# Passages between the parts of a decoder layer in a written order, with the output projection run one token tile after the other

## The chip, the cores and the metric

The kernel runs on one core of a Trainium2 chip. The metric is the device time of one execution in microseconds (us); for the kernel before there are three timed runs and one profiled execution. The engines are named as in the profile: PE (TensorE, matrix products and transposes), DVE (VectorE), ACT (ScalarE), POOL (GpSimd) and SP (SyncE, which issues the loads).

## The reference, cut to what matters

A trunk of two decoder layers on 256 tokens with model width 1024 in float32.

```python
def hybrid_layer(x, ...):
    h = rms_norm(x, attn_pre_gain)
    u = h @ w_in                                  # 1024 -> 4120 columns
    o_a = swa_sink_attention(qa, ka, va, sinks)   # from the columns of u
    o_b = nsa_attention(...)                      # compressed, selected, window
    mixed = sigmoid(g_a) * (o_a @ w_branch_a) + sigmoid(g_b) * (o_b @ w_branch_b)
    x = x + rms_norm(mixed @ w_out, attn_post_gain)
    h = rms_norm(x, ffn_pre_gain)
    x = x + rms_norm(conv_ffn(h, ffn_w_up, conv_w, conv_b, ffn_w_down), ffn_post_gain)
    return x

def conv_ffn(h, w_up, conv_w, conv_b, w_down):    # d_ff = 2816
    u = h @ w_up                                  # 1024 -> 2 * 2816
    c = conv_b + sum(conv_w[k] * (u shifted by 2 - k tokens) for k in range(3))
    a, val = split(c, 2)
    return (gelu(a) * val) @ w_down
```

rms_norm(x, g) is x * rsqrt(mean(x * x) + eps) * g. The change concerns three places: from `mixed @ w_out` to the FFN's up-projection, the last columns of the FFN, and from the FFN's end to the next layer's `h @ w_in`.

## The kernel before, in words

The 256 tokens are two tiles t of 128, which lie on the partitions. The residual stream X stays on chip. Every float32 factor is split into a hi part (rounded to the matmul's format, a copy on ACT, L114) and a lo part (the rest, a subtraction on DVE, L117), and each product is three matmuls that add up in one PSUM bank: hi x hi, hi x lo and lo x hi (`mm3`, L376 to L378). A normalised activation is transposed by PE in groups of four 128x128 blocks (`t4`, L383), and the transposed tile is split in the same way.

All weights pass once through a stream `W`. A chunk is 512 KB: SP loads it into one of four slots "st", ACT makes hi, DVE makes lo. hi and lo go into the rings "wh" and "wl" of four slots each, or into other homes that happen to be free: "kB" (one), "sg" (two), "q8" (three). `W.next` hands out the next chunk and makes chunks ahead of use by the number `ahead` of each; `W.make(i)` makes a certain one early, and `W.high(i)` makes the hi part and returns the function for the lo part.

PSUM has eight banks under four names, two each: "mm", "S", "O", "T". In tiles of the profile's rows the name stands without its number.

The program is written part by part (`part`), and `later(n, fn)` puts work n parts later. Within it a scheduler sets each engine's order, except in blocks under `tc.manual_schedule`, where the engines keep the written order. What matters here, layer by layer:

- `out_layer`, the output projection: 8 chunks k of w_out, 128 rows by 1024 columns; for each chunk and tile six matmuls into two banks (`res[0]` is O, `res[1]` is S). `post_norm` and `after` make the mean square on ACT (L372), the gain on DVE (L401), rstd on POOL (L364, L365), X on DVE (L407), the mean square of X, X times the next gain (L974), rstd again, and the scaled rows xg (L981). `t8` transposes xg into the pair `hp` of "q8" homes.
- `ffn_layer`: the first two column pairs are computed with tokens on the partitions (`up_first`, four chunks into a bank "mm" for each tile) and transposed. The other pairs j = 2 to 21 have the columns on the partitions (`up`, L1022 to L1024, 24 matmuls of 256 columns for each of two halves), then the convolution (L1007 to L1009), gelu (L1031), the product (L1035), its split, and `down` with LAG pairs' delay: six matmuls for each tile into S (t = 0) and O (t = 1).
- At the end of the FFN the products of pairs 18 to 21 remain for both tiles. w_down chunks 20 and 21 lie in "kB" and "sg", 18 and 19 in the ring. Then `post_norm`, `gained` (L415) and the transposes to the next layer's `xp`, and `in_tile(0)` with its four chunks of w_in.

The order of the output projection's products before (t, k), with tile 0's last two between tile 1's first ones:

```python
order = [(0, k) for k in range(6)] + [(1, 0), (1, 1), (0, 6), (1, 2), (0, 7), (1, 3), (1, 4), (1, 5), (1, 6), (1, 7)]
```

Of the kernel before, what the change touches and what calls it, by code (L numbers as in the profile page):

```python
# [65 lines left out]
def tile_hybrid_trunk(  # L66
# [49 lines left out]
    def sub(dst, a, b):  # L116
        dve.tensor_tensor(dst, a, b, ALU.subtract)  # L117
# [270 lines left out]
    def t8(src, pair, t):  # L388
        tk = slice(t * P, (t + 1) * P)
        for h in range(2):  # L390
            t4(src[:, h * 512:(h + 1) * 512], pair[0][:, h * 4:h * 4 + 4, tk], pair[1][:, h * 4:h * 4 + 4, tk])

    def behind(ins):
        return nullcontext() if ins is None else tc.issue_after(ins.ins)

    def post_norm(t, banks, gain, follow=None, after=None):
        s2 = mean_sq(banks)
# [1 line left out]
        with behind(after):
            for n in range(2):  # L400
                dve.tensor_tensor(g[n], banks[n], gain[:, n * 512:(n + 1) * 512], ALU.mult)  # L401
        r = rstd_of(s2)
        last = None
        for n in range(2):
            xs = X[:, t, n * 512:(n + 1) * 512]
            with behind(last):
                dve.scalar_tensor_tensor(xs, g[n], r, xs, ALU.mult, ALU.add)  # L407
            if follow:
                last = follow(n)
        return last  # L410
# [858 lines left out]
```

## Time and profile before

| | us |
|---|---|
| timed runs | 784.13, 784.28, 782.39; median 784.13 |
| profiled execution, device time | 782.81 |
| its span in the trace | 781.0 |
| busy: PE, DVE, ACT, POOL | 759.2, 613.1, 495.4, 34.0 |
| weights and inputs read | 129.37 MB, 167 GB/s over the span |

The span runs from the first to the last instruction of the profiled execution; the device time has 1.8 us around it. A row of the timeline reads: start, duration, engine, line, operation, out<-in, shape, count, and in brackets the idle time before it with what ended it. In a list of waits a row names who waited for whom, the total, the times and the longest. Matmuls overlap in the pipeline, so their spacing from start to start is their price, not the duration in the row. The granted clock of PE was 0.998.

### The profile page before, as it was taken

The page shows a single profiled execution, that of the slowest core. Times are in us where ns is not written, and L with a number is a line of the kernel's source. Part 1 is how long each engine was busy: PE and PEld are TensorE (multiplying, and loading weights), DVE is VectorE, ACT ScalarE, POOL GpSimd, SP SyncE. Part 2 cuts the span into 40 slices and gives each one's busy share as a digit, 9 for nine tenths or more (in the row PEclk, how much of TensorE's full clock was granted, in tenths as well). Part 3 has the DMA queues.
Part 4 walks back from the last instruction along what each step waited for, and adds up shares of the span by engine and source line. Part 5 has one row for each costly group of instructions (what it writes and reads, how often), then busy time and mean ns, then how long its engine had stood idle before and what let it go on. Part 6 is the DMA issues. An engine that isn't in the chain of part 4 may idle for free.

```text
span 781.0 us, 12886 instructions
## 1 busy us (share of the span) xinstructions
PE 759.2 (97%) x4742; PEld 676.8 (87%) x4742; DVE 613.1 (79%) x1188; ACT 495.4 (63%) x950; POOL 34.0 (4%) x60
## 2 busy tenths in 40 slices
PE   8999999999899999999989999999999999999996
PEld 6788898887799999999868889988878999999995
DVE  6899898686787777777787989985876877677775
ACT  6596986754665555565556969866465655566552
POOL 4300001000100000000010000010010000000000
PEclk9999999999999999999999999999999999999999
DMA  8624264465566565665545323644645556656731
GB/s 337 196 86 133 64 219 170 136 188 162 173 205 189 188 187 184 209 210 188 164 134 163 95 82 121 200 153 162 200 144 172 188 187 189 188 182 201 217 104 54
DMA packets 42346, 131.26 MB, mean 168 GB/s; under 512 B 5375, under 2 KB 5931, under 8 KB 42283
## 3 DMA queue, kind: packets, MB, share of 16 engines
q1 hardware_dynamic: 41707, 129.39, 52.0%
q10 hardware_dynamic: 576, 1.05, 0.4%
q8 instruction: 37, 0.61, 0.3%
q14 instruction: 26, 0.21, 0.1%
HBM read 129.37 MB, written 1.05 MB: 167 GB/s over the span
## 4 chain that ended last, share of the span: by engine, by line
PE 83%; ACT 8%; DVE 4%; POOL 2%; issue 1%; DMA 1%; SPq 0%; DVEq 0%; POOLq 0%; ACTq 0%
PE mm L376 6%; PE mm L378 6%; PE mm L377 6%; PE T L1024 5%; PE mm L1023 5%; PE T L1023 5%; PE mm L1024 5%; PE T L1022 5%; PE mm L1022 5%; PE S L377 5%; PE S L376 5%; PE S L378 5%; PE O L376 3%; PE O L377 3%; PE O L378 3%; ACT k L635 2%
## 5 line engine op out<-in xcount | busy, mean ns | idle before, releaser
L117 DVE TENSOR_TENSOR wl<-st,wh 128x1024 fp32r<-128x1024 f32 (+2 forms) x220 | 260.4, 1186 | 101.5 <-ACT wh L114 100.3
L114 ACT ACTIVATE wh<-st 128x1024 fp32r<-128x1024 f32 (+2 forms) x220 | 225.5, 1028 | 178.1 <-PE O L378 40.5
L376 PE MATMUL mm<-wh,x 128*128 128x512 f32 (+2 forms) x248 | 92.9, 375 | 0.7 <-DVE VT L546 0.6
L377 PE MATMUL mm<-wl,x 128*128 128x512 f32 (+2 forms) x248 | 91.6, 370 | 0.0
L378 PE MATMUL mm<-wh,x 128*128 128x512 f32 (+2 forms) x248 | 91.3, 368 | 0.1
L1023 PE MATMUL mm<-q,wh 128*128 128x256 f32 x320 | 90.7, 284 | 0.0
L1024 PE MATMUL T<-q,wl 128*128 128x256 f32 x320 | 90.6, 283 | 0.0
L1023 PE MATMUL T<-q,wh 128*128 128x256 f32 x320 | 90.6, 283 | 0.0
L1024 PE MATMUL mm<-q,wl 128*128 128x256 f32 x320 | 90.6, 283 | 0.0
L1022 PE MATMUL T<-q,wh 128*128 128x256 f32 x320 | 90.5, 283 | 0.0
L1022 PE MATMUL mm<-q,wh 128*128 128x256 f32 x320 | 90.5, 283 | 0.0
L1022 PEld LDWEIGHTS mm<-q,wh 128*128 128x128 f32 x320 | 61.4, 192 | 0.9
L1022 PEld LDWEIGHTS T<-q,wh 128*128 128x128 f32 x320 | 61.4, 192 | 0.8
L1023 PEld LDWEIGHTS mm<-q,wh 128*128 128x128 f32 x320 | 61.4, 192 | 0.8
L1023 PEld LDWEIGHTS T<-q,wh 128*128 128x128 f32 x320 | 61.4, 192 | 0.7
L1024 PEld LDWEIGHTS mm<-q,wl 128*128 128x128 f32 x320 | 61.4, 192 | 0.1
L1024 PEld LDWEIGHTS T<-q,wl 128*128 128x128 f32 x320 | 61.4, 192 | 0.0
L378 PEld LDWEIGHTS mm<-wh,x 128*128 128x128 f32 x248 | 46.7, 188 | 6.1 <-DVE x L117 0.5
L376 PEld LDWEIGHTS mm<-wh,x 128*128 128x128 f32 x248 | 46.7, 188 | 6.0 <-issue 0.8
L377 PEld LDWEIGHTS mm<-wl,x 128*128 128x128 f32 x248 | 46.7, 188 | 4.8
L635 ACT ACTIVATE k<-k,mn 128x128 f32<-128x128 f32 (+1 forms) x96 | 42.4, 445 | 7.1 <-DVE mn L632 7.0
L114 ACT ACTIVATE k<-k 128x256 fp32r<-128x256 f32 x72 | 29.1, 413 | 9.1 <-DVE k L1035 5.6
(294 smaller groups left out, 1657.0 us busy)
## 6 DMA issues: line engine op xcount, KB each, us to landing
st<-in_ffn_w_up_dram SPq DMA_DIRECT2D x88, 512.0 KB, 4.2
st<-in_ffn_w_down_dram SPq DMA_DIRECT2D x44, 512.0 KB, 3.9
st<-in_w_in_dram SPq DMA_DIRECT2D x42, 512.0 KB, 3.6
st<-in_w_out_dram SPq DMA_DIRECT2D x16, 512.0 KB, 3.8
st<-in_w_in_dram SPq DMA_DIRECT2D x16, 384.0 KB, 3.1
st<-in_cmp_w_dram SPq DMA_DIRECT2D x16, 256.0 KB, 2.6
st<-in_w_branch_a_dram SPq DMA_DIRECT2D x8, 512.0 KB, 3.6
st<-in_w_branch_b_dram SPq DMA_DIRECT2D x8, 512.0 KB, 3.5
```

The costliest lines, as they stand in the source:

```text
L114: return act.activation(dst, src, AF.Copy, scale=scale)
L117: dve.tensor_tensor(dst, a, b, ALU.subtract)
L376: pe.matmul(o, xh, wh, start=first, stop=False, skip_group_check=True)
L377: pe.matmul(o, xh, wl, start=False, stop=False, skip_group_check=True)
L378: pe.matmul(o, xl, wh, start=False, stop=last, skip_group_check=True)
L635: last_exp[0] = act.activation(self.pt[:, hh, s, :], sm[:, :nk], AF.Exp, bias=self.mn[:, i:i + 1], scale=-1.0, accum_out=self.dn[:, i:i + 1])
L1022: pe.matmul(o, wh[:, k, :], hh[:, k, c0:c1], start=(k == 0), stop=False, skip_group_check=True)
L1023: pe.matmul(o, wh[:, k, :], hl[:, k, c0:c1], start=False, stop=False, skip_group_check=True)
L1024: pe.matmul(o, wl[:, k, :], hh[:, k, c0:c1], start=False, stop=(k == 7), skip_group_check=True)
```

## The change

- The output projection runs tile 0 through all eight chunks (banks O), then tile 1 in the order 2, 0, 1, 3, 4, 5, 6, 7 (banks S). All eight chunks are kept: 5 in a new pair of homes "split" (the tiles "kA" and "vbd"), 6 in "sg", 7 in "q8". The first up-projection chunk goes into "kB" instead of "q8".
- From the second product on, PE, DVE and ACT follow the written order until the first product of tile 1 of `up_first`. The norm is written out as `norm_a`, `norm_b` and `scaled`; `scaled` does gain and rstd in one instruction. Tile 0's transposes stand behind the fifth and the sixth chunk of tile 1, tile 1's transposes behind tile 0 of `up_first` (`last_T`).
- `up_first` does hi x hi for both k of a chunk, then hi x lo, then lo x hi.
- The last pair j = 21 is taken out of the loop: its first half has the bank "T", its second a bank "mm" of its own, in written order, and so is the rest of the passage to the next layer: all products of tile 0, then tile 1's, with tile 0's transposes ahead of and behind the last chunk, and tile 1's transposes inside `in_tile(0)` of the next layer. In the last layer the written order ends before the products.
- Chunks 0 and 1 of layer 1's w_in are made at pairs 15 and 17 of layer 0 and kept in "q8" and "split"; chunks 2 and 3 are made in the passage.

The order's names below are a tile's short name with a number where several are alive; the first operand of a product is the weight. **DVE, tile 1's norm in the output projection of layer 0.** wl are lo parts of up-projection chunks, q the transposed activations, k_610 to k_613 (after: k_611 to k_621) the norm's rows. Before:

```order
L117 TENSOR_TENSOR wl_2363<-st_2360,wh_2362 128x1024
L117 TENSOR_TENSOR wl_2375<-st_2372,wh_2374 128x1024
L117 TENSOR_TENSOR wl_2434<-st_2431,wh_2433 128x1024
L117 TENSOR_TENSOR q_570_2216<-T_2384,q_569_2215 128x4x128
L117 TENSOR_TENSOR q_570_2216<-T_2391,q_569_2215 128x4x128
L401 TENSOR_TENSOR k_610_2408<-S_2213,gain_1994 128x512
L401 TENSOR_TENSOR k_611_2409<-S_2214,gain_1994 128x512
L407 SCALAR_TENSOR_TENSOR X<-k_610_2408,rstd_2412,X 128x512
L407 SCALAR_TENSOR_TENSOR X<-k_611_2409,rstd_2412,X 128x512
L974 TENSOR_TENSOR k_613_2417<-X,gain_2209 128x512 x2
L981 TENSOR_SCALAR k_613_2417<-k_613_2417,rstd_2426 128x512 x2
```

After:

```order
L117 TENSOR_TENSOR q_586_2300<-T_2365,q_585_2299 128x4x128
L117 TENSOR_TENSOR q_586_2300<-T_2378,q_585_2299 128x4x128
L117 TENSOR_TENSOR wl_2388<-st_2385,wh_2387 128x1024
L117 TENSOR_TENSOR wl_2394<-st_2391,wh_2393 128x1024
L402 TENSOR_TENSOR k_611_2411<-S_2213,gain_1994 128x512
L402 TENSOR_TENSOR k_612_2412<-S_2214,gain_1994 128x512
L407 SCALAR_TENSOR_TENSOR X<-k_611_2411,rstd_2417,X 128x512
L407 SCALAR_TENSOR_TENSOR X<-k_612_2412,rstd_2417,X 128x512
L117 TENSOR_TENSOR wl_2423<-st_2420,wh_2422 128x1024
L978 SCALAR_TENSOR_TENSOR k_621_2437<-X,rstd_2434,gain_2209 128x512 x2
```

In front of the norm (L401, after: L402) stood three lo parts and the split of tile 0's transposes; now the split comes first and two lo parts stand behind it; one lo part moves between X and the scaled rows, and L974 and L981 are one instruction, L978.

**ACT, the last pairs of layer 0's FFN.** k_902, k_916 and k_927 (after: k_904, k_918, k_926) are the first halves of pairs 19, 20 and 21, wh the hi parts: wh_4326 (after: wh_4337) is w_down chunk 18, wh_4356 (after: wh_4373) chunk 19, and wh_4414, wh_4432 before are w_in chunks. Before:

```order
L114 ACTIVATE wh_4326<-st_4324 128x1024
L114 ACTIVATE k_904_4226<-k_902_4216 128x256
L114 ACTIVATE wh_4356<-st_4354 128x1024
L1007 ACTIVATE k_916_4309<-T_4248,vec 128x256
L114 ACTIVATE wh_4414<-st_4412 128x1024
L1031 ACTIVATE k_916_4309<-k_916_4309 128x256
L1007 ACTIVATE k_917_4314<-T_4248,vec 128x256
L114 ACTIVATE wh_4432<-st_4430 128x1024
L114 ACTIVATE k_918_4319<-k_916_4309 128x256
L1007 ACTIVATE k_927_4384<-T_4323,vec 128x256
L1031 ACTIVATE k_927_4384<-k_927_4384 128x256
L1007 ACTIVATE k_928_4389<-T_4323,vec 128x256
```

After:

```order
L114 ACTIVATE wh_4337<-st_4335 128x1024
L114 ACTIVATE k_906_4235<-k_904_4225 128x256
L1041 ACTIVATE k_918_4318<-T_4257,vec 128x256
L1067 ACTIVATE k_918_4318<-k_918_4318 128x256
L1041 ACTIVATE k_919_4323<-T_4257,vec 128x256
L114 ACTIVATE k_920_4328<-k_918_4318 128x256
L1041 ACTIVATE k_926_4365<-T_4334,vec 128x256
L1145 ACTIVATE k_926_4365<-k_926_4365 128x256
L114 ACTIVATE wh_4373<-st_4371 128x1024
L1041 ACTIVATE k_931_4401<-mm_4370,vec 128x256
L114 ACTIVATE wh_4405<-st_4403 128x1024
L114 ACTIVATE k_935_4411<-k_926_4365 128x256
```

Chunk 19 stood directly ahead of pair 20's first convolution; it now stands behind convolution and gelu of pair 21 (L1145), and the two w_in chunks that stood between the convolutions are later (others of them: wh_4405) or were made in earlier pairs.

**PE, the end of the products of layer 0 and the first of layer 1.** S and O are the products' banks of tile 0 and 1, k_939 (after: k_947) the rows of tile 0 for the next layer, x their transposes, sg chunk 21 of w_down. Before:

```order
L378 MATMUL O_2649<-kB_3756,k_919_4320 128x512
L376 MATMUL O_2648<-sg_3947,k_929_4394 128x512
L377 MATMUL O_2648<-sg_3948,k_929_4394 128x512
L378 MATMUL O_2648<-sg_3947,k_930_4395 128x512
L376 MATMUL O_2649<-sg_3947,k_929_4394 128x512
L377 MATMUL O_2649<-sg_3948,k_929_4394 128x512
L378 MATMUL O_2649<-sg_3947,k_930_4395 128x512
L383 MATMUL T_4483<-cst,k_939_4442 128x128 x4
L383 MATMUL T_4490<-cst,k_939_4442 128x128 x4
L376 MATMUL mm_4529<-wh_4414,x_931_4398 128x512
```

After:

```order
L384 MATMUL O_2647<-kB_3754,k_921_4329 128x512
L389 MATMUL T_4489<-cst,k_947_4459 128x128 x4
L382 MATMUL O_2646<-sg_3950,k_935_4411 128x512
L383 MATMUL O_2646<-sg_3951,k_935_4411 128x512
L384 MATMUL O_2646<-sg_3950,k_936_4412 128x512
L382 MATMUL O_2647<-sg_3950,k_935_4411 128x512
L383 MATMUL O_2647<-sg_3951,k_935_4411 128x512
L384 MATMUL O_2647<-sg_3950,k_936_4412 128x512
L389 MATMUL T_4513<-cst,k_947_4459 128x128 x4
L382 MATMUL mm_4541<-q_845_3852,x_940_4422 128x512
```

Both transposes of tile 0 stood behind tile 1's last product; now one stands ahead of its last chunk and one behind, and the next layer's first chunk comes from a home "q8" instead of the ring.

The diff, cut to its core:

```diff
+            elif tag == "split":
+                hi = ap_.tile([P, a, b], F32R, tag="kA", name=nm("kA"))
+                lo = ap_.tile([P, a, b], F32R, tag="vbd", name=nm("vbd"))
...
-                W.add(w_in[l, off:off + 2 * P * w].rearrange("(p k n) -> p k n", p=P, k=2), 2, w,
-                      ahead=0 if i == 1 and c < 2 or i == 0 and l == 0 else AH[i])
+                at_home = {0: "q8", 1: "split"}.get(c, "w") if i == 0 and l else "w"
+                n = W.add(w_in[l, off:off + 2 * P * w].rearrange("(p k n) -> p k n", p=P, k=2), 2, w, at_home,
+                          ahead=0 if i == 1 and c < 2 or i == 0 else AH[i])
+                if i == 0:
+                    early[l, "in", c] = n
...
         for k in range(8):
-            W.add(wo[:, k:k + 1, :], 1, D, {2: "kB", 5: "sg"}.get(k, "w"), ahead=1 if k > 5 else 2)
+            W.add(wo[:, k:k + 1, :], 1, D, {2: "kB", 5: "split", 6: "sg", 7: "q8"}.get(k, "w"), ahead=2 if k < 3 else 0)
...
         for c in range(4):
-            W.add(wu[c].rearrange("p (k n) -> p k n", k=2), 2, 512, "q8" if c == 0 else "w", ahead=0)
+            W.add(wu[c].rearrange("p (k n) -> p k n", k=2), 2, 512, "kB" if c == 0 else "w", ahead=0)
...
-    def out_layer(l, yp, gains):
+    def out_layer(l, yp, gains, order):
...
-                mm3(res[t][n], yp[0][:, k, tk], yp[1][:, k, tk], w[0][:, 0, nn], w[1][:, 0, nn], k == 0, k == 7)
-            if k == 7:
-                after(t)
...
+        def product(t, ks):
+            for k in ks:
+                part(lambda: go(t, k))
...
+        def scaled(t, r):
             for n in range(2):
                 c = slice(n * 512, (n + 1) * 512)
...
+                dve.scalar_tensor_tensor(xg[t][:, c], X[:, t, c], r, gf[:, c], ALU.mult, ALU.mult)
...
+        seq = list(range(8)), [2, 0, 1, 3, 4, 5, 6, 7]
+        gf, gp = gains["ffn_pre"], gains["attn_post"]
+        xg = {}
+        first = W.used
+        product(0, [0])
+        order.enter_context(tc.manual_schedule(engines=MANUAL0))
+        for k in range(1, 8):
+            if k < 6:
+                W.make(first + k + 2)
+            product(0, [k])
+        hp = big8("q8", 3), big8("q8", 3)
+        g, r = norm_a(res[0], gp)
+        product(1, seq[1][:1])
+        low = W.high(first + 8)
+        for n in range(2):
+            norm_b(0, n, g, r)
+        r = rstd_of(mean_sq(halves(X[:, 0, :])))
+        low()
+        xg[0] = k4()
+        low = W.high(first + 9)
+        scaled(0, r)
+        low()
+        product(1, seq[1][1:5])
+        t4_of(xg[0], hp, 0, 0)
+        product(1, seq[1][5:6])
+        t4_of(xg[0], hp, 0, 1)
+        W.make(first + 10)
+        W.make(first + 11)
+        product(1, seq[1][6:])
+        g, r = norm_a(res[1], gp)
+        low = W.high(first + 12)
+        for n in range(2):
+            norm_b(1, n, g, r)
+        low()
+        s2 = mean_sq(halves(X[:, 1, :]))
+        if TG:
+            table(AF.Gelu_apprx_tanh)
+        r = rstd_of(s2)
+        xg[1] = k4()
+        scaled(1, r)
+        return hp, [lambda: t4_of(xg[1], hp, 1, 0), lambda: t4_of(xg[1], hp, 1, 1)]
...
-            for k in range(2):
-                kk = 2 * c + k
-                mm3(ub[t], hh[:, kk, tk], hl[:, kk, tk], uw[c][0][:, k, :], uw[c][1][:, k, :], kk == 0, kk == 7)
+
+            for a, b in ((0, 0), (0, 1), (1, 0)):
+                for k in range(2):
+                    kk = 2 * c + k
+                    pe.matmul(ub[t], hp[a][:, kk, tk], uw[c][b][:, k, :], start=(kk == a == b == 0), stop=(kk == 7 and a == 1), skip_group_check=True)
...
-                W.make()
+                if t == 0:
+                    for fn in last_T:
+                        fn()
+                later(2 if t == 0 else 1, lambda: up_first_T(t, us))
...
         for t in range(2):
             for c in range(4):
                 part(lambda: up_first(t, c))
-        for j in range(2, NJ):
+                if (t, c) == (1, 0):
+                    order.close()
+        for j in range(2, NJ - 1):
             for half in range(2):
                 part(lambda: up(j, half, 0, T))
             for half in range(2):
                 act_gate(j, half)
             if j in (NJ - 8, NJ - 6):
                 W.make(early[l, NJ - 1 if j == NJ - 6 else NJ - 2])
+            if not last and j in (NJ - 7, NJ - 5):
+                W.make(early[l + 1, "in", 1 if j == NJ - 5 else 0])
...
+        j = NJ - 1
+        order.enter_context(tc.manual_schedule(engines=MANUAL0))
+        part(lambda: up(j, 0, 0, T))
+        ca = conv(up_bank.pop(j), j, 0)
+        act.activation(ca, ca, AF.Gelu_apprx_tanh)
+        up_bank[j] = bank("mm")
+        part(lambda: up(j, 1, 0, T))
+        nxt = None if last else [early[l + 1, "in", c] for c in range(4)]
+        cv = conv(up_bank.pop(j), 22 + j, 1, None if last else lambda: lows.append(W.high(nxt[2])))
+        dve.tensor_tensor(ca, ca, cv, ALU.mult)
+        gh, gl = k1(F32R), k1(F32R)
+        copy(gh, ca)
+        sub(gl, ca, r32(gh))
+        gs[j] = (gh, gl)
...
+        js = range(NJ - 4, NJ)
+
+        def downs(t, js, ns=(0, 1)):
+            for j in js:
+                part(lambda: down(j, t, ns))
...
+            order.close()
+            downs(0, js)
+            after(0)
+            downs(1, js[:2])
+            for n in range(2):
+                downs(1, js[2:], (n,))
+            after(1)
+            return None, rs, []
+        lows.append(W.high(nxt[3]))
+        for f in lows:
+            f()
+        xp = big8("x8", 2), big8("x8", 2)
+        xg = [None, None]
+
+        def update(t, g, r):
+            xg[t] = k4()
+            for n in range(2):
+                norm_b(t, n, g, r)
...
+        downs(0, js)
+        update(0, *norm_a(banks[0], gains["ffn_post"]))
+        downs(1, js[:3])
+        t4_of(xg[0], xp, 0, 0)
+        downs(1, js[3:])
+        g, r = norm_a(banks[1], gains["ffn_post"])
+        t4_of(xg[0], xp, 0, 1)
+        update(1, g, r)
+        return xp, rs, [lambda: t4_of(xg[1], xp, 1, 0), lambda: t4_of(xg[1], xp, 1, 1)]
```

More of the change, by code (lines that the diff above doesn't have):

```diff
@@ L386, in t4, with norm_a, norm_b, post_norm @@
         sub(dst_lo, bv, r32(dst_hi))
[L388 to L397, printed above, removed]
-        g = [k2(), k2()]
[L399 to L403, printed above, removed]
-        for n in range(2):
[L405 to L410, printed above, removed]
+    def norm_a(banks, gain):
+        s2 = small("s2", 2, 6)
+        j = k4()
+        g = [k2(), k2()]
+        for n in range(2):
+            c = slice(n * 512, (n + 1) * 512)
+            act.activation(j[:, c], banks[n], AF.Square, scale=1.0 / 32.0, accum_out=s2[:, n:n + 1])
+            dve.tensor_tensor(g[n], banks[n], gain[:, c], ALU.mult)
+        return g, rstd_of(s2)
+    def norm_b(t, n, g, r):
+        xs = X[:, t, n * 512:(n + 1) * 512]
+        dve.scalar_tensor_tensor(xs, g[n], r, xs, ALU.mult, ALU.add)
+    def post_norm(t, banks, gain, follow):
+        g, r = norm_a(banks, gain)
+        for n in range(2):
+            norm_b(t, n, g, r)
+            follow(n)
+    def t4_of(src, pair, t, h):
+        t4(src[:, h * 512:(h + 1) * 512], pair[0][:, h * 4:h * 4 + 4, t * P:(t + 1) * P], pair[1][:, h * 4:h * 4 + 4, t * P:(t + 1) * P])
     def gained(xg, t, gain, n):
@@ L429, in first_split, with attn_layer @@
         return lambda: sub(pair[1][:, h * 4:h * 4 + 4, tk], m, r32(ho))
-    def attn_layer(l, xp, rs, gains, first):
+    def attn_layer(l, xp, rs, gains, first, order, last_T):
         xh, xl = xp
@@ L472, in go @@
                     W.make()
-            order = FIRST if first and i == 0 else [(t, c) for t in range(2) for c in range(4)] if tmajor else [(t, c) for c in range(4) for t in range(2)]
-            for t, c in order:
+            todo = FIRST if first and i == 0 else [(t, c) for t in range(2) for c in range(4)] if tmajor else [(t, c) for c in range(4) for t in range(2)]
+            for t, c in todo:
                 for fn in hooks.get((t, c), ()):
@@ L893, in attn_layer @@
         else:
[L894 removed]
+            in_tile(0, "mm", fin_a, tmajor=True, hooks={(0, 3): [last_T[0]], (1, 0): [last_T[1]], (1, 1): [order.close]})
         in_tile(1, "S", fin_b)
@@ L982, in after @@
-            later(DL["h0"] if t == 0 else DL["h1"], lambda: t8(xg, hp, t))
-        order = [(0, k) for k in range(6)] + [(1, 0), (1, 1), (0, 6), (1, 2), (0, 7), (1, 3), (1, 4), (1, 5), (1, 6), (1, 7)]
-        for t, k in order:
-            part(lambda: go(t, k))
-            if (t, k) in ((0, 7), (1, 4), (1, 5), (1, 7)):
-                W.make()
-        return hp
-    def ffn_layer(l, hp, gains, last):
+                dve.scalar_tensor_tensor(xg[t][:, c], X[:, t, c], r, gf[:, c], ALU.mult, ALU.mult)
@@ L1002, in down_bank, with conv @@
             return banks[t]
-        def conv(b, jj, half):
+        lows = []
+        def conv(b, jj, half, then=None):
             c = k1()
@@ L1096, in ffn_layer @@
                     part(lambda: down(j - LAG, t))
-        order = [(NJ - 4, 0), (NJ - 3, 0), (NJ - 2, 0), (NJ - 4, 1), (NJ - 1, 0), (NJ - 3, 1), (NJ - 2, 1), (NJ - 1, 1)]
-        rs = [None, None]
-        order_ = [None]
-        xp = None if last else (big8("x8", 2), big8("x8", 2))
-        def after(t):
-            if last:
-                ov = out[0].rearrange("(t p) d -> p t d", p=P)[:, t, :]
-                post_norm(t, banks[t], gains["ffn_post"], lambda n: nc.sync.dma_start(halves(ov)[n], halves(X[:, t, :])[n]) and None)
-                return
-            xg = k4()
-            order_[0] = post_norm(t, banks[t], gains["ffn_post"], lambda n: gained(xg, t, halves(gains["attn_pre"]), n), order_[0] if OA else None)
-            rs[t] = rstd_of(mean_sq(halves(X[:, t, :])))
-            if TE and t == 1:
-                with tc.issue_after(last_sq[0].ins):
-                    table(AF.Exp)
-            later(DL["x0"] if t == 0 else DL["x1"], lambda: t8(xg, xp, t))
@@ new lines, in ffn_layer @@
+        lows.append(W.high(nxt[3]))
[5 more added lines that the diff above has]
+            xg[t] = k4()
+            for n in range(2):
+                norm_b(t, n, g, r)
+                gained(xg[t], t, halves(gains["attn_pre"]), n)
+            rs[t] = rstd_of(mean_sq(halves(X[:, t, :])))
+        downs(0, js)
+        update(0, *norm_a(banks[0], gains["ffn_post"]))
+        downs(1, js[:3])
+        t4_of(xg[0], xp, 0, 0)
```

52 lines of the change are left out of this document (14 added, 38 removed).

## The prediction

> **What bounds the kernel now.** I read the page's head first, then the waits of PE, then the timelines of PE, DVE, ACT and POOL around the two longest waits.
>
> ```profile
> span 781.0 us, 12886 instructions
> PE 759.2 (97%) x4742; PEld 676.8 (87%) x4742; DVE 613.1 (79%) x1188; ACT 495.4 (63%) x950; POOL 34.0 (4%) x60
> PE   8999999999899999999989999999999999999996
> PEclk9999999999999999999999999999999999999999
> ```
>
> PE is busy for 759.2 of 781.0 us at an undisturbed clock, and the change keeps its matmuls. So only PE's pauses can be won. The list of what PE waited for begins with four groups that lie in the passages:
>
> ```profile
> PE T L383 <- DVE k L415: 2.9, 2, 1.6
> PE mm L378 <- DVE q L117: 2.8, 2, 1.4
> PE T L383 <- DVE k L981: 1.8, 4, 0.5
> PE mm L376 <- ACT q L114: 0.5, 2, 0.3
> ```
>
> The columns are us in total, times, longest. L415 is the passage from layer 0 to layer 1; the other three occur alike in both layers between output projection and FFN. Together they are 8.0 us, about 1% of the span: the change can win little more than that. PE's rows of layer 0's passage (start, us):
>
> ```profile
> 173.12 0.39 PE L376 MATMUL O<-wh,x 128*128 128x512 f32 x1
> 189.08 0.39 PE L378 MATMUL O<-wh,x 128*128 128x512 f32 x1
> 192.03 0.39 PE L376 MATMUL S<-sg,x 128*128 128x512 f32 x1
> 192.26 0.39 PE L377 MATMUL S<-sg,x 128*128 128x512 f32 x1
> 192.48 0.39 PE L378 MATMUL S<-sg,x 128*128 128x512 f32 x1
> 195.38 1.06 PE L383 MATMUL T<-cst,k 128*128 128x128 f32 x8 [0.46 <-DVE k L981]
> 196.20 0.48 PE L376 MATMUL S<-wh,x 128*128 128x512 f32 x1
> 197.44 0.40 PE L378 MATMUL S<-wh,x 128*128 128x512 f32 x1
> 205.41 1.06 PE L383 MATMUL T<-cst,k 128*128 128x128 f32 x8 [0.45 <-DVE k L981]
> 206.73 0.50 PE L376 MATMUL mm<-q,q 128*128 128x512 f32 x1 [0.25 <-ACT q L114]
> ```
>
> Three things are to be seen. A 512-column matmul costs 0.229 us from start to start (192.03 to 192.48), eight transposes 0.82 (195.38 to 196.20). From 173.12 to tile 1 of the up-projection (206.73) there are 48 O, 48 S and 24 mm matmuls and six groups of four transposes: 120 x 0.229 + 6 x 0.41 = 30.0 us, where 33.6 pass: 3.6 lost. And tile 0's last product ends late, at 189.47 (189.08 + 0.39), since 18 products of tile 1 stand ahead of it.
>
> **Part 1, output projection to FFN (twice).** The old order waits for chunks 6 and 7: their hi copies go into ring slots that free only when products have run. ACT's row of chunk 6, SP's issue of both loads, and their group on the page (us to landing last):
>
> ```profile
> 183.86 1.06 ACT L114 ACTIVATE wh<-st 128x1024 fp32r<-128x1024 f32 x1 [1.25 <-PE S L378]
> 172.42 3.26 SPq L159 DMA_DIRECT2D st<-in_w_out_dram  x2
> st<-in_w_out_dram SPq DMA_DIRECT2D x16, 512.0 KB, 3.8
> ```
>
> With homes for all eight, tile 0 can run through: 173.12 + 48 x 0.229 + 2 x 0.41 + 0.16 for the last one's tail = 185.1, 4.4 us earlier. What it needs is chunk 7, at 173.12 + 42 x 0.229 + 0.82 = 183.6. Its load is the second of the two issued from 172.42 to 175.68; landing 3.8 us after 175.4 gives 179.2, hi (1.06) and lo (1.2) behind it some 182.0: 1.6 us to spare. No stall, but little room.
>
> The norm chain from the last product to the first transpose took 195.38 - 189.47 = 5.9 us before. Rows of its links on ACT, DVE and POOL, of tile 0 and tile 1:
>
> ```profile
> 188.83 0.60 ACT L372 ACTIVATE k<-O 128x512 f32<-128x512 f32 x1 [2.55 <-PE O L378]
> 191.29 1.41 DVE L407 SCALAR_TENSOR_TENSOR X<-k,rstd,X 128x512 f32<-128x512 f32 x2 [0.37 <-POOL rstd L365]
> 194.74 0.88 DVE L981 TENSOR_SCALAR k<-k,rstd 128x512 f32<-128x512 f32 x2 [0.83 <-POOL rstd L365]
> 195.54 3.49 DVE L117 TENSOR_TENSOR wl<-st,wh 128x1024 fp32r<-128x1024 f32 x3
> 200.15 1.28 DVE L401 TENSOR_TENSOR k<-S,gain 128x512 f32<-128x512 f32 x2
> 204.19 0.55 POOL L365 TENSOR_TENSOR rstd<-rstd,neg_half 128x1 f32<-128x1 f32 x1
> ```
>
> After: 185.1 + 5.9 = 191.0. PE reaches that transpose after five chunks of tile 1, at 184.9 + 30 x 0.229 = 191.8: no wait. L974 and L981 become one instruction of about 1.41 (as L407, the same form, took); L974 lay beside the squares of X and L981 (0.88 for both halves) on the path, so the path gets 0.5 us more work, of which the first transposes wait for half, and the eight instructions that go win nothing. The second transposes come one chunk later, and up-projection of tile 0, which before stood 1.4 us for the lo half (DVE had three subtractions, 3.49 us, ahead of it), now finds hi and lo split during the last two chunks: 0.
>
> Tile 1 ends its products at 173.12 + 96 x 0.229 + 4 x 0.41 + 0.2 = 197.0. Its chain took 205.41 - 197.84 = 7.6 us before, because DVE reached L401 only at 200.15. Now two lo subtractions, of up chunks 2 and 3, stand ahead of it; their hi copies follow the split of the second transposes (194.1) on ACT: 0.6 + 2 x 1.06, then 1.2 for the second lo, 198.2 with the hand-overs: L401 to 199.6, L407 to 201.0, squares of its second half 0.6, POOL 1.2, scaled's first half 0.7: transpose at 203.6. PE is done with tile 0 of the up-projection at 196.8 + 24 x 0.229 = 202.3. A wait of 1.35 is left, then 0.25 for the second half and about 0.15 of restarts: of 3.6 us lost, 1.8 stay, 1.8 are won. Bounds: with the first chain's 5.9 us the transposes stand at 202.9 and 2.7 are won; with 7.6 us 1.0 is won. I take 1.8, the walk in between; layer 1 has the same order, so **3.6 for both (2.0 to 5.4)**.
>
> **Part 2, layer 0 to layer 1.** PE, then ACT and DVE:
>
> ```profile
> 378.68 0.39 PE L376 MATMUL S<-wh,k 128*128 128x512 f32 x1
> 391.68 0.65 PE L383 MATMUL T<-cst,k 128*128 128x128 f32 x4 [1.58 <-DVE k L415]
> 393.60 0.66 PE L383 MATMUL T<-cst,k 128*128 128x128 f32 x4 [1.27 <-DVE k L415]
> 394.01 0.48 PE L376 MATMUL mm<-wh,x 128*128 128x512 f32 x1
> 373.00 1.06 ACT L114 ACTIVATE wh<-st 128x1024 fp32r<-128x1024 f32 x1 [1.49 <-PE T L1023]
> 376.84 0.40 ACT L1031 ACTIVATE k<-k 128x256 f32<-128x256 f32 x1
> 380.03 0.55 ACT L1007 ACTIVATE k<-T,vec 128x256 f32<-128x256 f32 x1
> 382.42 0.42 ACT L1031 ACTIVATE k<-k 128x256 f32<-128x256 f32 x1 [1.84 <-DVE k L1009]
> 383.32 0.48 DVE L1008 SCALAR_TENSOR_TENSOR k<-T,vec,k 128x255 f32<-128x255 f32 x1 [1.00 <-ACT k L1007]
> 385.54 1.22 DVE L117 TENSOR_TENSOR wl<-st,wh 128x1024 fp32r<-128x1024 f32 x1 [0.76 <-ACT wh L114]
> ```
>
> From 378.68 to the next layer's first product PE has 48 matmuls and two groups of transposes, 48 x 0.23 + 0.82 = 11.9, and takes 15.3: 3.4 lost. The new order runs all of tile 0 first and hides its chain behind tile 1; two banks let the last pair's first conv start about 2.9 us earlier (one half, 24 matmuls of 0.12).
>
> A new wait comes in. In ACT's fixed row the hi copy of w_down chunk 19, which ran at 373.00, stands behind conv and gelu of pair 21. Pair 20's conv takes that place: 373.0 + 0.55, two DVE steps of 0.48, gelu 0.40, conv 0.55, three DVE steps, copy 0.40: 377.3. Pair 21's conv, its DVE steps behind the copy's subtraction, gelu: 379.3. Then hi 380.4, lo 381.7. PE wants hi at 378.68 + 6 x 0.23 = 380.1 and lo at 380.3: it stands some 1.4 us. Queued behind the copy on ACT are the second conv and w_in chunks 2 and 3, behind the lo on DVE the second conv's steps and pair 21's product; its hi split comes at 383.6, and the delayed PE wants it at 384.3. Tile 0 ends at 378.68 + 24 x 0.23 + 1.4 = 385.6 (before 387.8); its chain, with DVE's two lo subtractions ahead of L401, gives the gained halves at 389.6 and 391.0; PE asks at 389.8 and 391.6: no wait. Layer 1 begins at 378.68 + 11.9 + 1.4 = 392.0 instead of 394.01: 2.0 won, less some 0.3 for later transposes behind a busy DVE: **1.7**. Bounds: if gelu of pair 21 is as late as it was (382.42), 3.5 us after the walk's 378.9, lo comes as much later and -1.8 is left; if PE waits for nothing, 3.4 are won.
>
> **Part 3, what costs nothing.** Layer 1's last pair gets the same two banks, but the scheduler orders the products behind it, and tile 1's fill a wait for chunk 19; PE then ends as before, so I take 0, at worst the 1.4 us of layer 0. The two w_in tiles made earlier go into layer 0's pairs 15 and 17, with their two loads on SP, which leave the transition:
>
> ```profile
> 316.00:350.00 34.00, 34.00 (x241) 31.96 (x240) 27.33 (x40) 20.62 (x30) 0.00 (x0) 1.00 0.71 217
> st<-in_ffn_w_up_dram SPq DMA_DIRECT2D x88, 512.0 KB, 4.2
> L1022 PEld LDWEIGHTS mm<-q,wh 128*128 128x128 f32 x320 | 61.4, 192 | 0.9
> ```
>
> In these 34.0 us (first row; columns: PE, PEld, DVE, ACT, POOL, clock, DMA share, GB/s) DVE is busy 27.3; two subtractions add 2.4, ACT's 20.6 gains 2.1, DMA 1 MB at a share of 0.71. PE, busy throughout, covers all of it; without that cover DVE's 2.4 would show.
>
> The regrouped products of the up-projection no longer have two neighbours with one stationary operand. By the rows above, hi x hi to hi x lo (same operand, 192.03 to 192.26) takes 0.23, hi x lo to lo x hi (another) 0.22; and the page counts as many loads as matmuls (4742 each). Cost 0. [...] This trace contradicts that a load is shared here.
>
> **Sum.** -3.6 - 1.7 = -5.3. Against the profiled execution's 782.81 us (span plus 1.8) that is 777.5; against the median 784.13, 0.17% higher, 778.8. I say 778.4. About 0.3%, 2.35 us, is what a measurement of this kernel tells from no change.
>
> **Rivals.**
> - *All passages close.* Chunk 19 is ready in time and tile 1's chain is as short as tile 0's: 5.4 + 3.4 = 8.8, so 774 to 775. For it: PE hides everything else of that kind. Against it: the row on ACT. Chance 0.16.
> - *New waits take the old ones' place.* Both chains at 7.6 us (2.0 won in all) and chunk 19's copy at the late bound (-1.8): 0.2 won, 783.9; the case runs up to 3.5 won, and somewhat under half of it lies above 2.35 us. For it: a fixed row can't slip another product in. Against it: ahead of tile 1's L401 stand two lo subtractions instead of three. Chance 0.14.
> - *Slower: the weight ring in pairs 14 to 17.* Four tiles instead of three now pass four slots in 8.5 us. A slot is held for landing 4.2, hi 1.06 and lo 1.22, 6.5 us. It decides once landing exceeds 6.2 us: each of 16 tiles then adds its excess, and 0.5 us more apiece gives 8.0 lost, 2.7 net: 787. For it: share 0.71 rises to about 0.8. Against it: 4.2 was measured at this load. Chance 0.05.
> - *Loads were shared.* 8 pairs x 2 tiles x 2 layers = 32 further loads, of 192 ns each (the load row above) if nothing hid them, 6.1 us: net +0.8, 784.9, no change. [...] Chance 0.01, after the equal spacings.
>
> **Chances and range.** The forecast has 0.64 (gain 3.5 to 7). Faster: 0.64 + 0.16 + 0.06 = 0.86; same 0.10; slower 0.04. The range reaches from nearly all closed (784.13 - 8.8 - 0.5 = 774.8) to just no change told (781.8).
>
> **What would show it.** Right: tile 0's last O product near 185, no wait on L978 for tile 0, one of about 1.4 for tile 1, and the mm wait of 1.39 gone; in the transition a wait of S for ACT's or DVE's chunk 19 near 380, no 1.58 and 1.27. Wrong: a wait on chunk 7 near 183, pair 21's conv late, PE pauses between 300 and 350, matmul spacing over 0.23 in the up-projection.

## Result and the profile after

The changed kernel takes 777.34 us (four runs, 777.25 to 778.14) against 783.91 us of the kernel before (four runs, 782.39 to 784.28): ratio 0.9922, 95% interval 0.9905 to 0.9939, 6.6 us faster by the medians and 5.1 by the lowest runs. The forecast was 778.4 with 774.8 to 781.8. The head of the page and the first rows of what PE waited for, with the changed kernel's own line numbers (L389 is the transposes' line, L978 the scaled rows, L117 the lo parts, L114 the hi parts):

```profile
span 775.5 us, 12867 instructions
PE 758.0 (98%) x4742; PEld 677.1 (87%) x4742; DVE 610.6 (79%) x1180; ACT 494.7 (64%) x950; POOL 33.4 (4%) x60
...
PE T L389 <- DVE k L978: 2.3, 2, 1.2
...
PE S L383 <- DVE wl L117: 0.8, 1, 0.8
...
PE S L382 <- ACT wh L114: 0.4, 1, 0.4
```

PE does the same 4742 matmuls; 5.5 us of the span are gone. The four groups of waits in the passages, 8.0 us together, are replaced by three, 3.5 us. In all PE's idle time fell by 4.3 us (21.8 to 17.5), and its busy time by 1.2, as there are fewer waits: the matmul behind a wait costs 0.34 us from start to start (379.76 to 380.10) instead of 0.23. Layer 0's first passage and the transition on PE (start, us):

```profile
184.56 0.39 PE L384 MATMUL O<-q,x 128*128 128x512 f32 x1
...
191.60 0.60 PE L389 MATMUL T<-cst,k 128*128 128x128 f32 x4
...
196.40 0.39 PE L384 MATMUL S<-q,x 128*128 128x512 f32 x1
...
203.38 1.29 PE L389 MATMUL T<-cst,k 128*128 128x128 f32 x8 [1.16 <-DVE k L978]
204.70 1.66 PE L1099 MATMUL mm<-kB,q 128*128 128x512 f32 x6
...
378.50 0.49 PE L382 MATMUL S<-wh,k 128*128 128x512 f32 x1 [0.40 <-ACT wh L114]
...
379.76 0.50 PE L383 MATMUL S<-wl,k 128*128 128x512 f32 x1 [0.77 <-DVE wl L117]
...
387.99 0.60 PE L389 MATMUL T<-cst,k 128*128 128x128 f32 x4
...
389.83 0.60 PE L389 MATMUL T<-cst,k 128*128 128x128 f32 x4
390.19 0.48 PE L382 MATMUL mm<-q,x 128*128 128x512 f32 x1
```

Tile 0's last product starts at 184.56 (189.08 before), its transposes wait for nothing, and only tile 1's transposes wait. In the transition the old waits of 1.58 and 1.27 are gone and chunk 19 has taken their place with 0.40 and 0.77. To see where the time went, I set the start of every matmul against the start of the same one, by number, in the trace of before. The shift is -0.19 us from the first products on (the start of a run differs by up to 0.4 us between any two traces), -2.13 after layer 0's passage, unchanged to 0.01 us through pairs 3 to 20, -4.16 at layer 1's first products and -3.66 once its first tile runs, -5.60 after layer 1's passage and -5.53 at the end. So the parts are -1.94, -1.53, -1.94 and +0.07 us.

### The profile page after: what moved, and what is told of

Same layout as the page of the kernel before. It is cut to its first block, busy times and chain, and to the rows that moved or that the text cites. A ratio compares the mean times of both kernels' runs of the same rounds, so it can differ in the third digit from the quotient of the medians.

```text
span 775.5 us, 12867 instructions
## 1 busy us (share of the span) xinstructions
PE 758.0 (98%) x4742; PEld 677.1 (87%) x4742; DVE 610.6 (79%) x1180; ACT 494.7 (64%) x950; POOL 33.4 (4%) x60
## 4 chain that ended last, share of the span: by engine, by line
PE 83%; ACT 7%; DVE 5%; issue 2%; POOL 1%; DMA 1%; SPq 0%; DVEq 0%; POOLq 0%; ACTq 0%
PE mm L382 6%; PE mm L384 6%; PE mm L383 6%; PE mm L1060 5%; PE mm L1059 5%; PE mm L1058 5%; PE S L383 5%; PE S L384 5%; PE S L382 5%; PE T L1060 5%; PE T L1059 5%; PE T L1058 5%; PE O L383 4%; PE O L382 4%; PE O L384 4%; PE T L668 2%
## 5 line engine op out<-in xcount | busy, mean ns | idle before, releaser
L117 DVE TENSOR_TENSOR wl<-st,wh 128x1024 fp32r<-128x1024 f32 (+2 forms) x214 | 253.3, 1185 | 95.3 <-ACT wh L114 94.8
L114 ACT ACTIVATE wh<-st 128x1024 fp32r<-128x1024 f32 (+2 forms) x214 | 218.7, 1026 | 155.1 <-PE mm L1059 37.7
L1058 PE MATMUL mm<-q,wh 128*128 128x256 f32 x336 | 95.1, 283 | 0.0
L1059 PE MATMUL mm<-q,wh 128*128 128x256 f32 x336 | 95.1, 283 | 0.0
L1060 PE MATMUL mm<-q,wl 128*128 128x256 f32 x336 | 95.0, 283 | 0.0
L382 PE MATMUL mm<-wh,x 128*128 128x512 f32 (+2 forms) x240 | 89.7, 374 | 0.7 <-DVE VT L552 0.6
L383 PE MATMUL mm<-wl,x 128*128 128x512 f32 (+2 forms) x240 | 88.3, 368 | 0.0
L384 PE MATMUL mm<-wh,x 128*128 128x512 f32 (+2 forms) x240 | 88.2, 367 | 0.0
L1060 PE MATMUL T<-q,wl 128*128 128x256 f32 x304 | 86.0, 283 | 0.0
L1059 PE MATMUL T<-q,wh 128*128 128x256 f32 x304 | 86.0, 283 | 0.0
L1058 PE MATMUL T<-q,wh 128*128 128x256 f32 x304 | 85.9, 283 | 0.0
L1058 PEld LDWEIGHTS mm<-q,wh 128*128 128x128 f32 x336 | 64.4, 192 | 0.9
L1059 PEld LDWEIGHTS mm<-q,wh 128*128 128x128 f32 x336 | 64.4, 192 | 0.8
L1058 PEld LDWEIGHTS T<-q,wh 128*128 128x128 f32 x304 | 58.3, 192 | 0.8
L1059 PEld LDWEIGHTS T<-q,wh 128*128 128x128 f32 x304 | 58.3, 192 | 0.7
L382 PEld LDWEIGHTS mm<-wh,x 128*128 128x128 f32 x240 | 45.2, 188 | 5.7 <-issue 0.8
L384 PEld LDWEIGHTS mm<-wh,x 128*128 128x128 f32 x240 | 45.1, 188 | 5.6 <-DVE x L117 0.4
L383 PEld LDWEIGHTS mm<-wl,x 128*128 128x128 f32 x240 | 45.2, 188 | 4.5
L114 ACT ACTIVATE k<-k 128x256 fp32r<-128x256 f32 x72 | 29.1, 413 | 17.4 <-DVE k L1071 7.6
```

The costliest lines, as they stand in the source:

```text
L114: return act.activation(dst, src, AF.Copy, scale=scale)
L117: return dve.tensor_tensor(dst, a, b, ALU.subtract)
L382: pe.matmul(o, xh, wh, start=first, stop=False, skip_group_check=True)
L383: pe.matmul(o, xh, wl, start=False, stop=False, skip_group_check=True)
L384: pe.matmul(o, xl, wh, start=False, stop=last, skip_group_check=True)
L1058: pe.matmul(o, wh[:, k, :], hh[:, k, c0:c1], start=(k == 0), stop=False, skip_group_check=True)
```

## The experiments

The kernels below were timed on three chips, each with runs of the kernel before beside them, whose lowest were 782.36 (the first four kernels below), 782.18 (the next four) and 782.60 us (the last two). So times of two of these kernels, or of one and the changed kernel's 777.34 us, can differ by some 0.4 us for that reason alone, and the shift between the traces is the finer measure: in the five traces that share a passage to the FFN its shift agrees within 0.08 us.

**One half of the change alone, twice.** First the output projection with its homes and both passages to the FFN:

```diff
-        for j in range(2, NJ - 1):
+        for j in range(2, NJ):
...
-        j = NJ - 1
-        order.enter_context(tc.manual_schedule(engines=MANUAL0))
...
+        todo = [(NJ - 4, 0), (NJ - 3, 0), (NJ - 2, 0), (NJ - 4, 1), (NJ - 1, 0), (NJ - 3, 1), (NJ - 2, 1), (NJ - 1, 1)]
...
-                at_home = {0: "q8", 1: "split"}.get(c, "w") if i == 0 and l else "w"
+                at_home = "w"
```

> The changed output projection, its homes and its norm with both passages to the FFN; the end of the FFN and the passage from layer 0 to layer 1 as before. My theory (each passage's own wait is won, and they add): -1.94 us in each layer by the shift between the two traces, so 3.9 us faster than before, ratio 0.995, about 779.9, with the 1.58 and 1.27 waits of the transition back. Rival (the parts help each other: the transition only gains since the out passage frees homes or DVE time): less than 2.5 us.

Measured 779.46 us, ratio to before 0.9948 (0.9930 to 0.9965). By the shift of matmuls the two passages give -1.90 and -1.97 us. My theory holds; but the trace has something I had not looked for, of which below: in this execution the transition is 1.2 us slower than in the trace of before, with the same two waits (1.57 and 1.27 us).

The other half:

```diff
-        seq = list(range(8)), [2, 0, 1, 3, 4, 5, 6, 7]
+        order = [(0, k) for k in range(6)] + [(1, 0), (1, 1), (0, 6), (1, 2), (0, 7), (1, 3), (1, 4), (1, 5), (1, 6), (1, 7)]
...
-            W.add(wo[:, k:k + 1, :], 1, D, {2: "kB", 5: "split", 6: "sg", 7: "q8"}.get(k, "w"), ahead=2 if k < 3 else 0)
+            W.add(wo[:, k:k + 1, :], 1, D, {2: "kB", 5: "sg"}.get(k, "w"), ahead=1 if k > 5 else 2)
```

(The old body of `out_layer`, the old `up_first` and the old homes come with it.)

> The other half alone: last pair in two banks, the passage from layer 0 to layer 1 in written order and the two early w_in chunks; the output projection and the passage to the FFN as before. My theory: 1.5 us faster than before, ratio 0.998, about 782.3, with the wait for chunk 19 (0.4 and 0.8) near the end of layer 0's FFN and the waits of 0.46, 1.39, 0.45 and 0.25 back in both layers. Rival (parts help each other): no gain, or over 2.5 us.

Measured 781.28 us, ratio 0.9968 (0.9956 to 0.9979). By the shift the transition gives -1.54 and nothing else moves; chunk 19's waits are there and the four old ones of the out passages are back. The product of both ratios is 0.9916, the whole change has 0.9922, and the shifts of the passages are those of the whole change: the parts add up, and none needs the other. Within the first half the order of the products, the homes and the written order of the engines were not run apart, so how its 3.9 us divide among them stays open.

**The order of the products with one stationary operand.**

```diff
-            for a, b in ((0, 0), (0, 1), (1, 0)):
-                for k in range(2):
-                    kk = 2 * c + k
-                    pe.matmul(ub[t], hp[a][:, kk, tk], uw[c][b][:, k, :], start=(kk == a == b == 0), stop=(kk == 7 and a == 1), skip_group_check=True)
+            for k in range(2):
+                mm3(ub[t], hh[:, kk, tk], hl[:, kk, tk], uw[c][0][:, k, :], uw[c][1][:, k, :], kk == 0, kk == 7)
```

> The changed kernel with the first up-projection's products in the old order, hi x hi, hi x lo, lo x hi for each k, so that two neighbours have one stationary operand. My theory (every matmul loads its own operand): the same time as the changed kernel within 0.3 us, spacing 0.227 us. Rival (a load serves both neighbours, 32 loads of 0.19 us): up to 6.1 us faster than the changed kernel, about 771.

Measured 777.39 us, 0.05 from the changed kernel. The up-projection's rows (L382 and L383 have the same stationary operand, L384 another):

```profile
196.85 0.39 PE L382 MATMUL mm<-kB,q 128*128 128x512 f32 x1
197.07 0.39 PE L383 MATMUL mm<-kB,q 128*128 128x512 f32 x1
197.30 0.39 PE L384 MATMUL mm<-kB,q 128*128 128x512 f32 x1
197.53 0.39 PE L382 MATMUL mm<-kB,q 128*128 128x512 f32 x1
```

0.22, 0.23, 0.23, and the page of before, which has this order too, counts 4742 loads for 4742 matmuls: no load is shared, and the regrouping cost nothing. By the shift it even wins 0.12 to 0.16 us in each layer, little more than two traces of one passage differ by.

**Gain and rstd apart again.**

```diff
+        gain_x(t)
...
+            dve.tensor_tensor(xg[t][:, c], X[:, t, c], gf[:, c], ALU.mult)
...
-            dve.scalar_tensor_tensor(xg[t][:, c], X[:, t, c], r, gf[:, c], ALU.mult, ALU.mult)
+            dve.tensor_scalar(xg[t][:, c], xg[t][:, c], r, None, ALU.mult)
```

> The changed kernel with gain and rstd as two instructions again (eight more on DVE, about 2.5 us more busy) and the lo part that stood between X and the scaled rows of tile 1 behind them. My theory (tile 1's chain is on the path; the gain can run while the squares and rstd are formed, and only rstd's multiplication, 0.44 us for a half instead of 0.70, stays on it): the wait on the scaled rows falls from 1.16 to some 0.75 us, and 0.4 to 0.5 us are won in each layer, 0.9 in all, about 776.4. Rival (fewer DVE instructions are what helped): slower than the changed kernel by up to 2.5 us.

Measured 777.51 us: neither. By the shift it is 0.10 to 0.15 us slower in each layer. The wait on tile 1's rows did fall, to 0.95, but tile 0's transposes now wait too, and a wait costs more than its idle time: they start 0.55 us behind the matmul ahead of them (191.27), in the changed kernel 0.24 (191.36 to 191.60), for 0.16 us of idle time. Behind tile 1's transposes PE then waits 0.25 us for ACT's copy. Why tile 0's rows are late stands in POOL's row. First two rows of the changed kernel (POOL, DVE), then three of this one:

```profile
189.05 0.44 POOL L370 TENSOR_SCALAR rstd<-s 128x1 f32<-128x1 f32 x1 [2.31 <-ACT k L378]
188.10 1.22 DVE L117 TENSOR_TENSOR kB<-st,kB 128x1024 fp32r<-128x1024 f32 x1
```

```profile
188.95 1.56 POOL L370 TENSOR_SCALAR rstd<-s 128x1 f32<-128x1 f32 x1 [2.31 <-ACT k L378]
189.22 1.22 DVE L117 TENSOR_TENSOR kB<-st,kB 128x1024 fp32r<-128x1024 f32 x1
...
191.82 0.63 PE L389 MATMUL T<-cst,k 128*128 128x128 f32 x4 [0.16 <-DVE k L984]
203.44 0.74 PE L389 MATMUL T<-cst,k 128*128 128x128 f32 x5 [0.95 <-DVE k L984]
```

POOL's step on 128 numbers takes 1.56 us here and ends (190.51) 0.07 us after the DVE subtraction, which the extra gain has pushed to 189.22. In the changed kernel it ends (189.49) 0.17 us after the same subtraction (189.32). Over both passages to the FFN in the traces of before and of the changed kernel, and layer 0's in this one, the pattern is the same: where DVE works with two SBUF operands as this step arrives, it ends 0.15 to 0.17 us after DVE's instruction, 14 times of 15, and once, in this kernel, 0.07 us after the next one; where DVE reads a PSUM bank, it takes 0.30 or 0.31 us, 5 times of 5.

**The two early homes.**

```diff
-                at_home = {0: "q8", 1: "split"}.get(c, "w") if i == 0 and l else "w"
+                at_home = "w"
-            if not last and j in (NJ - 7, NJ - 5):
-                W.make(early[l + 1, "in", 1 if j == NJ - 5 else 0])
```

> The changed kernel without the two early homes: layer 1's first two w_in chunks go into the ring where chunks 2 and 3 stood, and 2 and 3 are made between the norms. My theory (two more lo parts in the passage stand ahead of the split of the transposes and of tile 1's norm on DVE): PE waits some 1.1 us for the first lo split and 0.3 later, 1.5 us slower than the changed kernel, about 778.9. Rival (the homes only move work that PE covers): same time as the changed kernel within 0.3 us.

Measured 779.13 us, 1.8 more than the changed kernel; by the shift the transition loses 1.95 us, more than all it had won. PE waits from 390.82 for the split behind a lo part (0.64 us), from 395.37 for the gained rows (0.50), and in the attention's transposes (0.49). Without the early chunks and their homes the transition wins nothing.

**One bank for the last pair.**

```diff
         part(lambda: up(j, 0, 0, T))
-        ca = conv(up_bank.pop(j), j, 0)
-        act.activation(ca, ca, AF.Gelu_apprx_tanh)
-        up_bank[j] = bank("mm")
         part(lambda: up(j, 1, 0, T))
+        ca = conv(up_bank[j], j, 0)
+        act.activation(ca, ca, AF.Gelu_apprx_tanh)
```

> The changed kernel with both halves of the last pair in one bank, in both layers; the order of writing then also puts the hi copy of w_down chunk 19 ahead of pair 20's convolution, where it was before. My theory (the gain of two banks is taken back by the later chunk 19, and pair 21's convolution has to wait for pair 20's chain on ACT and DVE in any case): no wait for chunk 19, some 0.7 us for pair 21's split instead; 0 to 0.8 us faster than the changed kernel. Rival (two banks are what lets the transition gain): its 1.5 us are lost, about 779.

Measured 776.24 us, 1.1 less than the changed kernel; by the shift -0.8 in the transition. ACT's rows from the end of pair 20 on, and PE's wait:

```profile
370.95 1.06 ACT L114 ACTIVATE wh<-st 128x1024 fp32r<-128x1024 f32 x1 [1.49 <-PE T L1059]
371.91 0.55 ACT L1041 ACTIVATE k<-T,vec 128x256 f32<-128x256 f32 x1
...
376.67 0.42 ACT L114 ACTIVATE k<-k 128x256 fp32r<-128x256 f32 x1 [1.52 <-DVE k L1071]
376.99 0.55 ACT L1041 ACTIVATE k<-T,vec 128x256 f32<-128x256 f32 x1
...
381.54 0.50 PE L382 MATMUL S<-sg,k 128*128 128x512 f32 x1 [0.57 <-ACT k L114]
```

Chunk 19 is split at 370.95 and PE has it in time. Pair 21's convolution starts at 376.99, right behind pair 20's copy: PE has done both halves by then (its last matmul of pair 21 ends at 376.79), so in this order the convolution would wait for pair 20 with two banks as well. By these rows the second bank brings nothing once chunk 19 stands ahead of pair 20 (two banks with chunk 19 ahead were not run), and this order is 0.8 us better than the changed kernel's, where chunk 19 stands behind pair 21's gelu.

**Chunk 20 ahead of chunk 19.**

```diff
+        for j in js:
+            wdn[j] = W.next(1, D)
-        downs(0, js)
+        downs(0, (NJ - 4, NJ - 2, NJ - 3, NJ - 1))
```

> The changed kernel with tile 0's last products of layer 0 in the order 18, 20, 19, 21. My theory (chunk 19's lo part comes at 379.7 on the changed kernel's clock, and chunk 20 lies ready in a home): the waits of 0.40 and 0.77 for chunk 19 go but for some 0.15, a wait of about 0.6 for pair 21's split takes their place, 0.4 to 0.6 us won. Rival (PE's wait there is covered by tile 0's chain later on): same time within 0.2 us at the first product of layer 1.

Measured 776.65 us; by the shift -0.65 in the transition. Of chunk 19's 1.17 us a wait of 0.03 is left, and 0.40 on pair 21's split has come. PE's wait there was on the path: what is taken from it arrives at layer 1's first product.

**Chunk 20 ahead and gain and rstd apart, together.**

> Gain and rstd apart and the products in the order 18, 20, 19, 21 together. If both act by themselves, 0.9 + 0.5 = 1.4 us faster than the changed kernel, about 775.9. If only the first does, 776.4.

Measured 776.89 us: by the shift the order of the chunks gives -0.70 in the transition, about as it did alone, and the apart norm takes back 0.17 and 0.20 us in the passages.

**Only what is on the path: the first half.** With POOL's row read, the next kernel puts ahead of rstd only the gain of tile 1's first half, so that DVE rests when POOL's step comes, and keeps one bank:

```diff
+        dve.tensor_tensor(xg[1][:, 0:512], X[:, 1, 0:512], gf[:, 0:512], ALU.mult)
...
+                if t == 1 and n == 0:
+                    dve.tensor_scalar(xg[1][:, c], xg[1][:, c], r, None, ALU.mult)
+                    continue
...
-        low()
...
         scaled(1, r)
+        low()
```

> The one-bank kernel, and in tile 1's norm of the output projection the gain of the first half of X ahead of rstd (0.69 us), then rstd times that half (0.44), the second half in one instruction as in the changed kernel, and the lo part that stood between X and the scaled rows behind them. My theory (POOL's first rstd step, 0.43 to 0.51 us there, ends 0.16 us after the DVE instruction with two SBUF operands that is in flight, and takes 0.3 with none in flight; PE waits for the first half alone): POOL's step falls to 0.3, the wait for the scaled rows from 1.16 to 0.75-0.8, 0.4 us won in each layer beside the one-bank kernel's 0.85: 1.6 us faster than the changed kernel, about 775.6. Rival (the wait is set by PE's second half or by ACT's table load): no faster than the one-bank kernel, 776.3.

Measured 775.72 us (775.51 to 775.83), ratio to before 0.9890 (0.9876 to 0.9905): the fastest of all. By the shift against the one-bank kernel the passages give -0.27 and -0.38 us, and the transition is the same. POOL, DVE and PE:

```profile
201.49 0.30 POOL L370 TENSOR_SCALAR rstd<-s 128x1 f32<-128x1 f32 x1 [2.57 <-ACT k L378]
...
202.46 0.49 DVE L983 TENSOR_SCALAR k<-k,rstd 128x512 f32<-128x512 f32 x1 [1.22 <-POOL rstd L371]
...
203.09 1.29 PE L389 MATMUL T<-cst,k 128*128 128x128 f32 x8 [0.76 <-DVE k L983]
```

POOL's step takes 0.30 and PE's wait falls from 1.16 to 0.76, as worked out; in layer 0 a part of the 0.4 us is given back within the next pairs.

**Extra matmuls in the old wait.** The slow transition in the trace of the first experiment shows in the windows of 2 us (columns: PE, PEld, DVE, ACT, POOL busy, PE's granted clock, DMA share, GB/s). That run first, then before, 2.2 us later on its clock:

```profile
388.00:390.00 2.00, 0.61 (x4) 0.42 (x4) 1.97 (x4) 1.35 (x5) 0.00 (x0) 1.00 0.58 207
390.00:392.00 2.00, 0.73 (x4) 0.68 (x4) 2.00 (x4) 1.62 (x5) 0.60 (x3) 0.81 0.01 2
392.00:394.00 2.00, 2.00 (x8) 1.61 (x7) 1.36 (x3) 0.60 (x1) 1.27 (x3) 0.50 0.52 150
394.00:396.00 2.00, 2.00 (x9) 1.66 (x8) 1.93 (x4) 0.85 (x3) 0.00 (x0) 0.83 0.32 113
```

```profile
390.00:392.00 2.00, 0.42 (x4) 0.33 (x4) 1.83 (x3) 1.07 (x3) 0.10 (x1) 1.00 0.72 225
392.00:394.00 2.00, 0.73 (x8) 0.49 (x6) 2.00 (x4) 1.90 (x7) 0.40 (x2) 1.00 0.05 18
394.00:396.00 2.00, 1.93 (x10) 1.32 (x9) 1.82 (x4) 0.60 (x1) 1.46 (x4) 1.00 0.42 123
```

PE has the same waits in both, but in the first its clock is halved behind them. PE's rows there:

```profile
389.39 0.66 PE L389 MATMUL T<-cst,k 128*128 128x128 f32 x4 [1.57 <-DVE k L446]
391.32 1.11 PE L389 MATMUL T<-cst,k 128*128 128x128 f32 x4 [1.27 <-DVE k L446]
...
393.09 0.63 PE L384 MATMUL mm<-wh,x 128*128 128x512 f32 x1
393.52 0.63 PE L382 MATMUL mm<-wh,x 128*128 128x512 f32 x1
```

The two groups of transposes take 0.66 and 1.11 us, and the matmuls are 0.43 us apart instead of 0.23. PE's clock of 0.81, 0.50 and 0.83 in the last three windows of the first table, with 1.00 ahead of them and behind, puts the fall to one half at 391.24 and the return at 394.68: some 3.4 us, more than the 2.5 that the test below names. So the kernel before got this test:

```diff
+                        fill = bank("mm")
+                        for _ in range(6):
+                            pe.matmul(fill, gs[NJ - 1][0][:, 0:P], wk[:, 0, 0:512], start=True, stop=True, skip_group_check=True)
```

> The kernel before, with six extra matmuls into a free bank (1.4 us, their result unused) in PE's wait of 1.58 us in the passage from layer 0 to layer 1. My theory (in some executions of the kernel before, PE's clock is halved for some 2.5 us after the two waits there, as in the profile of the run with the new output projection alone, which costs 1.2 us and makes the runs of the kernel before lie at 782.4 or at 784 to 785): with PE busy in the first of the waits no execution loses its clock, all runs lie within 0.5 us of 782.5, and the median is 0 to 1 us under that of the kernel before. Rival (the spread comes from the loads or elsewhere): the same spread up to 785.

Measured 782.69 us, twelve runs from 782.41 to 783.25; beside them 17 runs of the kernel before lay at 782.60 to 785.75, median 783.89; ratio 0.9982 (0.9973 to 0.9991). Six matmuls whose result nobody uses make the kernel before faster. One run lies outside the 0.5 us that I had set, and the median fell by 1.2 where I had set at most 1. In its profile the first wait is 0.19 us instead of 1.58 and the second the same:

```profile
389.78 1.57 PE L1135 MATMUL mm<-sg,k 128*128 128x512 f32 x6
391.54 0.66 PE L384 MATMUL T<-cst,k 128*128 128x128 f32 x4 [0.19 <-DVE k L416]
393.46 0.66 PE L384 MATMUL T<-cst,k 128*128 128x128 f32 x4 [1.27 <-DVE k L416]
```

The one trace of the kernel before does not show the fall, but each run has its mean granted clock. The 40 runs of before beside the experiments fall into three groups: 17 at 782.2 to 783.0 us with a mean clock of 0.997 to 0.999, 13 at 783.7 to 784.3 with 0.996, and 10 at 785.05 to 785.75 with 0.994 or 0.995. A stretch of 3.4 us at half clock takes 0.5 x 3.4 / 782 = 0.0022 from the mean, so by this estimate the groups have none, one and two such stretches. So the spread of the kernel before goes with its mean clock, by the estimate with a halved clock in some executions, and goes away with the filled wait (twelve runs at 0.997 to 0.999), and its median holds about 1.2 us of it.

## Why the prediction was right

- **Term 1, the two passages to the FFN, 3.6 us (2.0 to 5.4).** Measured 1.94 + 1.94 = 3.9. Tile 0's last product was set at 185.1 and ended at 184.95; on chunk 7 there was no wait; tile 1's wait was set at 1.35 and was 1.16; L1099 of tile 1 starts at 204.70 where the walk had 204.9. Two small errors cancelled, which is luck: a matmul costs 0.227 us instead of 0.229 (the two spacings shown for it even give 0.225), and a group of four transposes within the products 0.45 instead of 0.41. By the walk's own numbers the bounds for one layer, 2.7 and 1.0, come out 0.1 to 0.2 us lower.
- **Term 2, the transition, 1.7 us (-1.8 to 3.4).** Measured 1.53. The new wait for chunk 19 was set at 1.4 and was 1.17; layer 1's first product was set at 392.0 on before's clock and came at 390.19 + 2.13 = 392.3. By the shift 2.0 us are won at layer 1's first products, and 0.5 are given back in the transposes behind them, where the sum had 0.3. One reason given there did not hold: the two banks, which were to let the last pair's first convolution start 2.9 us earlier. With one bank the transition is 0.8 us faster still, so the gain does not need them; they came with the order that made chunk 19 late. Without the early chunks the gain is lost, and what the written order does by itself was not run.
- **Term 3, nothing.** Pairs 15 and 17 with the extra tiles shift by 0.00; the ring holds. The tail moved by 0.07.
- **The rivals.** That all passages close fell with the waits of 1.17 us for chunk 19 and of 1.16 for tile 1's rows; that new waits take the old ones' place fell with their sum, 3.5 us against 8.0; the ring fell with the shift that stays the same through pairs 3 to 20; shared loads fell with equal spacings and no change of time.
- **What the sum lacked.** Its 5.3 us stand against 5.5 in the two traces, but the medians differ by 6.6. The rest is put down to the reduced clock in some executions of before (a mean of 0.994 to 0.996 in 23 of the 40 runs), which its one trace does not show and which the changed kernel's runs (777.25 to 777.41, one at 778.14) hardly show: the lowest runs of both differ by 5.1 us, and filling one wait of before took 1.2 us from its median. The spread of the three runs, 782.39 to 784.28, was a hint of it; I read it as noise.
- **What the walk had wrong.** It took POOL's steps at the durations of before's rows; beside other work of DVE the first of them took from 0.30 to 1.56 us. And I priced the apart norm of the fourth experiment by DVE's times alone, 0.9 us won, where the traces show about 0.25 lost.
